# Seven products for eight in four of the eleven pairs of the last matrix product

## The chip, the cores and the metric

The kernel runs on one core of a Trainium2 chip. The metric is the device time of one execution in microseconds (us). TensorE (PE) multiplies; VectorE (DVE), ScalarE (ACT) and GpSimd (POOL) work on elements; SyncE (SP) issues most transfers.

## The reference

A trunk of two layers on 256 tokens of 1024 features, in float32. Each layer is half a SwiGLU step, a mixer, and another half step; at the end stands an RMS norm:

```python
def swiglu(h, w_gate, w_up, w_down):
    return (jax.nn.silu(h @ w_gate) * (h @ w_up)) @ w_down
...
    for layer in range(DEPTH):
        h = h + FFN_RESIDUAL_WEIGHT * swiglu(rmsnorm(h, ffn1_norm[layer]), ...)
        hn = rmsnorm(h, mix_norm[layer])
        ...
        h = h + FFN_RESIDUAL_WEIGHT * swiglu(rmsnorm(h, ffn2_norm[layer]), ...)
        ...
    return rmsnorm(h, final_norm)
```

The hidden width of SwiGLU is 2816 = 22 blocks of 128. The change concerns the last `swiglu` of layer 1 and its product with `w_down`, which is (256 x 2816) times (2816 x 1024).

## The kernel before, in words

**Numbers in two parts.** TensorE takes operands in a shorter format (`F32R`). So each operand is split: ScalarE copies it to a high part (`wh`, or half 0 of an `act` tile), VectorE subtracts that from the original for the low part (`wl`, half 1). A product is then three matmuls, high by high, high by low and low by high (`product`), or, for gate, up and the earlier down products, a wide matmul of 512 columns and a narrow one of 256 (`products_t`).

**Stages.** The stages follow each other: SwiGLU, mixer A, SwiGLU, SwiGLU, mixer B, SwiGLU, norm. Within the last SwiGLU (names `f21`), `ffn_blocks` goes over the 22 hidden blocks, two at a time. For each two it loads 1 MB of gate and 1 MB of up weights (`unit`: one transfer into a `raw` tile, then two high and two low tiles of 128 x 1024), and for each block it runs gate and up products and then closes the block before: join the two halves of the accumulator (ScalarE copy and VectorE add, `joined`), scale by the norm's row (VectorE for gate, GpSimd for up, L355), silu (ScalarE), multiply (L356), split into an `act` tile (`parts_of`). A list `beside` can hold calls that are put ahead of a double block.

**The last product.** `down_last` has the activations as the stationary operand and the weights as the moving one, so its result stands with tokens on the partitions. Two halves of 128 tokens (`t`) by two halves of 512 features (`c`) give four accumulators. It goes over 11 pairs of hidden blocks: one transfer of two rows of blocks (2 x 128 x 1024), split as above, then for each of two blocks k, each t and each c one product: eight products, 24 matmuls of 512 columns for a pair. The last two pairs (four blocks) are held back, so that the accumulators end one after the other: for each (t, c) the four blocks' products, then half of the result is added to the residual stream `h` (L432) and its squares and scaled outputs are begun (`finish_part`). The last accumulator is cut into two of 256 columns, the second of them called `end`.

**The residual stream** is kept with features on the partitions (`hT`). Ahead of `down_last` it is turned: 16 transposes of 128 x 128 on TensorE (L694) through three PSUM tiles (`trt`), and four ScalarE copies into `h[t][c]` (L695).

**What sets the order.** Each engine runs its own instructions in the order in which they are issued; a scheduler places them when the program is built, so this order is not quite that of the source. Buffers are pools: four `raw` tiles, eight tiles each of `wh` and `wl` (128 x 1024), 22 tiles "a" (`act` among them), five accumulators (`acc`) and three PSUM tiles (`trt`). A transfer waits until its `raw` tile has been split; a split waits until TensorE has read the part tile whose place it takes.

Of the kernel before, what the change touches and what calls it, by code (L numbers as in the profile page):

```python
# [25 lines left out]
NG = H // HG  # L26
ROT = 16
HALF = ROT // 2
LEAD = 4
EPS = 1e-6  # L30
SCALE = DH ** -0.5
# [31 lines left out]
def trunk(ctx: ExitStack, tc: tile.TileContext, a: dict, out: bass.AP):  # L63
# [13 lines left out]
    def atile(shape, dt=F32, name="a"):  # L77
        return ap_.tile(shape, dt, tag="a", name=name)

    def acc(name):  # L80
        return accp.tile([P, 512], F32, tag="acc", name=name)

    def flat(ap):
        return ap.rearrange("p c n -> p (c n)")

    def parts_of(hi, lo, src, scale=1.0, later=None):

        def rest():
            if isinstance(scale, float):
                nc.vector.tensor_sub(lo, src, hi.bitcast(F32))  # L90
# [9 lines left out]
    def trt(name):  # L100
        return trp.tile([P, 512], F32, tag="tr", name=name)
# [40 lines left out]
    def unit(name, k, n, srcs):  # L142

        raw = rawp.tile([P, k, n], F32, tag="raw", name=f"raw_{name}")
        for dst, src in srcs:
            nc.sync.dma_start(raw if dst is None else raw[:, :, dst], src)
        return pieces_of(name, raw, k, n)
# [28 lines left out]
    def rows(w, k0, k, c0, n):  # L176
        return w[k0 * P:(k0 + k) * P, c0:c0 + n].rearrange("(k p) n -> p k n", p=P)

    def product(accs, xh, xl, ws, first, last):

        for ac, (wh, wl) in zip(accs, ws):
            nc.tensor.matmul(ac, xh, wh, start=first, stop=False)  # L182
        for ac, (wh, wl) in zip(accs, ws):
            nc.tensor.matmul(ac, xh, wl, start=False, stop=False)  # L184
        for ac, (wh, wl) in zip(accs, ws):
            nc.tensor.matmul(ac, xl, wh, start=False, stop=last)  # L186
# [94 lines left out]
    class Pieces:  # L281
# [55 lines left out]
        nc.vector.tensor_add(s, ac[:, :S], s)  # L337
        return s

    def ffn_blocks(name, wg, wu, norm, first=None, beside=()):  # L340

        blocks = []

        def both(f, pair):
            acs = [acc(f"{name}_{n}{f}") for n in "gu"]
            cols = slice(f % 2 * P, (f % 2 + 1) * P)
            products_t(acs, [[(wh[:, cols], wl[:, cols]) for wh, wl in w] for w in pair], norm.x, True, True)
            return acs

        def close(f, gate, up):  # L350
            g = joined(gate, f"{name}_g{f}")
            nc.vector.tensor_mul(g, g, norm.row)  # L352
            nc.scalar.activation(g, g, AF.Silu)  # L353
            u = joined(up, f"{name}_u{f}")
            nc.gpsimd.tensor_tensor(u, u, norm.row, op=ALU.mult)  # L355
# [49 lines left out]
        down_t(name, wd, blocks, after)  # L405


    def down_last(name, w, nk, blocks, h, weight, part, after, tail=4):


        accs = [[acc(f"dn_{name}_{t}_{c}") for c in range(2)] for t in range(NT)]
        held = []

        def cut(ws, cols):
            return tuple(w[:, cols] for w in ws)

        halves = [slice(c * 512, (c + 1) * 512) for c in range(2)]
        for u in range(nk // 2):
            for i, ws in enumerate(unit(f"{name}_{u}", 2, D, [(None, rows(w, 2 * u, 2, 0, D))])):
                k = 2 * u + i  # L420
                if k < nk - tail:
                    for t in range(NT):
                        product(accs[t], *blocks[t][k], [cut(ws, half) for half in halves], k == 0, False)
                else:
                    held.append((k, ws))
        for t in range(NT):
            for c, half in enumerate(halves):
                n = 512 if (t, c) != (1, 1) else S
                for k, ws in held:
                    product([accs[t][c][:, :n]], *blocks[t][k], [cut(ws, slice(half.start, half.start + n))], False,  # L430
                            k == nk - 1)
                nc.vector.scalar_tensor_tensor(h[t][c], accs[t][c], weight, h[t][c], op0=ALU.mult, op1=ALU.add)  # L432
                part(t, slice(half.start, half.start + n))
            if t:
                end = acc(f"dn_{name}_end")[:, :S]
                for k, ws in held:
                    product([end], *blocks[t][k], [cut(ws, slice(D - S, D))], k == nk - tail, k == nk - 1)
                hc = h[1][1][:, S:]
                nc.vector.scalar_tensor_tensor(hc, end, weight, hc, op0=ALU.mult, op1=ALU.add)
                part(t, slice(D - S, D), True)  # L440
            after(t)

    def out_t(name, pieces, base, blocks, norm, tail=3):
# [224 lines left out]
    def ending(at):  # L668
# [18 lines left out]
    blocks = ffn_blocks("f21", a["ffn2_w_gate"][1], a["ffn2_w_up"][1], n6)  # L687

    h = [[xp.tile([P, 512], F32, tag=f"kx{2 * t + c}", name=f"h_{t}_{c}") for c in range(2)] for t in range(NT)]
    for t in range(NT):  # L690
        for c in range(2):
            tr = trt(f"h_{t}_{c}")
            for k in range(4):
                nc.tensor.transpose(tr[:, k * P:(k + 1) * P], hT[:, 4 * c + k, t * P:(t + 1) * P], ident)  # L694
            nc.scalar.activation(h[t][c], tr, AF.Copy)  # L695

    parts = [[], []]
    outs = [[None, None] for t in range(NT)]
# [26 lines left out]
    def finish(t):  # L725
# [8 lines left out]
    down_last("f21_d", a["ffn2_w_down"][1], KF,  # L734
              [[tuple(x[:, i, t * P:(t + 1) * P] for i in range(2)) for x in blocks] for t in range(NT)],
              h, 0.5, finish_part, finish)


_INS = ["ffn1_w_gate", "ffn1_w_up", "ffn1_w_down", "ffn2_w_gate", "ffn2_w_up", "ffn2_w_down",
# [23 lines left out]
```

## Time and profile before

| | |
|---|---|
| time, median of 3 runs | 990.88 us (990.67 to 990.91) |
| the profiled execution's own time | 990.92 us |
| its span, first to last instruction | 989.1 us |
| mean granted TensorE clock | 1.000 |
| 11 loads of the last product | 1024 KB each, 4.9 us from issue to landing (median) |
| HBM traffic | 177 GB/s over the span |

The lines of the profile are read so: a line number, an engine, an operation, the tile written and the tiles read with their numbers left out (so `f21_d` is shown as `f_d`), and the shape as partitions x elements. In a group, what follows the bar is the busy time, the mean length of one in ns, and the engine's idle time just before with what ended it. In a timeline the first column is the start and the second the length in us. Matmuls are pipelined: the length of one is longer than the distance to the next.

### The profile page before, as it was taken

To read this page: it belongs to the slowest core of one execution; us is meant where nothing else is said; L and a number is where in the kernel's file an instruction comes from. 1 tells how busy PE (TensorE), PEld (TensorE's weight loads), DVE (VectorE), ACT (ScalarE), POOL (GpSimd) and SP (SyncE) were. 2 spreads that over 40 slices of the span, in tenths; PEclk is the share of its full clock that TensorE was granted. 3 is DMA by queue.
4 is the path that set the end of the run, shared out by engine and by line. 5 is a ranking of instruction groups with operands and counts; after the bars stand their busy time and mean duration, and the time that the engine had idled before them with its cause. 6 is when DMAs were issued, how large, how long until landed. Compare 5 with 4: busy or idle time off the path is not lost.

```text
span 989.1 us, 15227 instructions
## 1 busy us (share of the span) xinstructions
PE 976.2 (99%) x5652; PEld 849.5 (86%) x5652; DVE 729.4 (74%) x1291; ACT 586.1 (59%) x1073; POOL 170.1 (17%) x194
## 2 busy tenths in 40 slices
PE   8999999999999999999999999999999999999997
PEld 5888888888889888888888888888888998888886
DVE  6987866677887788776678877656678878888642
ACT  7656654467776665655456566545577756665531
POOL 3211111122302211110112111101143022111000
PEclk9999999999999999999999999999999999999999
DMA  9776565655433566565655665665534345655611
GB/s 303 246 256 204 169 210 185 213 171 171 128 117 125 171 187 206 178 200 181 212 171 172 198 191 185 202 202 190 194 128 128 120 141 173 207 174 201 202 62 43
DMA packets 152395, 176.03 MB, mean 178 GB/s; under 512 B 3584, under 2 KB 140288, under 8 KB 152320
## 3 DMA queue, kind: packets, MB, share of 16 engines
q1 hardware_dynamic: 151600, 174.24, 55.1%
q8 instruction: 44, 0.72, 0.3%
q10 hardware_dynamic: 720, 0.82, 0.2%
q14 instruction: 31, 0.25, 0.1%
HBM read 173.99 MB, written 1.05 MB: 177 GB/s over the span
## 4 chain that ended last, share of the span: by engine, by line
PE 68%; DVE 2%; ACT 2%; issue 1%; POOL 0%; POOLq 0%; ACTq 0%; DVEq 0%
PE f_g L193 12%; PE f_u L193 12%; PE dn_f L193 8%; PE f_u L196 6%; PE f_g L196 6%; PE dn_f L196 4%; PE dn_f_d L186 2%; PE dn_f_d L182 2%; PE dn_f_d L184 2%; PE q_b L182 1%; PE kv_b L182 1%; PE q_b L186 1%; PE kv_b L186 1%; PE kv_b L184 1%; PE q_b L184 1%
## 5 line engine op out<-in xcount | busy, mean ns | idle before, releaser
L193 PE MATMUL f_g<-x_n,wh_f_g 128*128 128x512 f32 x688 | 180.1, 394 | 0.0
L193 PE MATMUL f_u<-x_n,wh_f_u 128*128 128x512 f32 x688 | 177.3, 390 | 0.0
L193 PEld LDWEIGHTS f_u<-x_n,wh_f_u 128*128 128x128 f32 x688 | 129.1, 188 | 27.3
L193 PEld LDWEIGHTS f_g<-x_n,wh_f_g 128*128 128x128 f32 x688 | 124.1, 189 | 22.7
L355 POOL TENSOR_TENSOR j_f_u<-j_f_u,r_n 128x256 f32<-128x256 f32 x88 | 77.6, 884 | 377.9 <-DVE j_f_u L337 355.5
L193 PE MATMUL dn_f<-act_f,wh_f 128*128 128x512 f32 x528 | 126.5, 391 | 0.0
L157 DVE TENSOR_TENSOR wl_f_u<-raw_f_u,wh_f_u 128x1024 fp32r<-128x1024 f32 x86 | 119.6, 1393 | 1.5 <-ACT wh_f_u L156 1.4
L157 DVE TENSOR_TENSOR wl_f_g<-raw_f_g,wh_f_g 128x1024 fp32r<-128x1024 f32 x86 | 103.6, 1235 | 15.1 <-PE f_g L196 10.7
L193 PEld LDWEIGHTS dn_f<-act_f,wh_f 128*128 128x128 f32 x528 | 96.8, 188 | 18.6
L157 DVE TENSOR_TENSOR wl_f<-raw_f,wh_f 128x1024 fp32r<-128x1024 f32 x72 | 81.8, 1153 | 35.6 <-ACT wh_f L156 26.7
L196 PE MATMUL f_u<-x_n,wl_f_u 128*128 128x256 f32 x688 | 103.3, 283 | 0.0
L196 PE MATMUL f_g<-x_n,wl_f_g 128*128 128x256 f32 x688 | 102.9, 282 | 0.0
L196 PEld LDWEIGHTS f_g<-x_n,wl_f_g 128*128 128x128 f32 x688 | 96.5, 190 | 6.3
L156 ACT ACTIVATE wh_f<-raw_f 128x1024 fp32r<-128x1024 f32 x72 | 67.3, 979 | 49.4 <-PE dn_f L193 27.1
L156 ACT ACTIVATE wh_f_g<-raw_f_g 128x1024 fp32r<-128x1024 f32 x86 | 89.4, 1049 | 11.2 <-issue 6.0
L156 ACT ACTIVATE wh_f_u<-raw_f_u 128x1024 fp32r<-128x1024 f32 x86 | 86.6, 1047 | 15.2 <-PE f_g L193 10.9
L196 PEld LDWEIGHTS f_u<-x_n,wl_f_u 128*128 128x128 f32 x688 | 91.6, 192 | 0.0
L230 POOL TENSOR_TENSOR ss_n<-ss_n,sq_n 128x256 f32<-128x256 f32 x42 | 41.9, 999 | 244.2 <-ACT sq_n L229 243.3
L94 ACT ACTIVATE act_f<-j_f_g 128x256 fp32r<-128x256 f32 x88 | 36.5, 417 | 72.1 <-DVE j_f_g L356 71.8
L353 ACT ACTIVATE j_f_g<-j_f_g 128x256 f32<-128x256 f32 x88 | 36.8, 418 | 67.1 <-DVE j_f_g L352 66.6
L196 PEld LDWEIGHTS dn_f<-act_f,wl_f 128*128 128x128 f32 x528 | 68.1, 191 | 2.8
L196 PE MATMUL dn_f<-act_f,wl_f 128*128 128x256 f32 x528 | 69.0, 283 | 0.0
(220 smaller groups left out, 1702.3 us busy)
## 6 DMA issues: line engine op xcount, KB each, us to landing
raw_f_g<-in_ffn_w_gate_dram SPq DMA_DIRECT2D x43, 1024.0 KB, 5.4
raw_f_u<-in_ffn_w_up_dram SPq DMA_DIRECT2D x43, 1024.0 KB, 5.3
raw_f<-in_ffn_w_down_dram SPq DMA_DIRECT2D x24, 1024.0 KB, 5.1
raw_f_d<-in_ffn_w_down_dram SPq DMA_DIRECT2D x11, 1024.0 KB, 4.9
raw_f<-in_ffn_w_down_dram SPq DMA_DIRECT2D x12, 768.0 KB, 4.5
raw_qka<-in_a_w_qkv_dram SPq DMA_DIRECT2D x16, 512.0 KB, 4.3
raw_va<-in_a_w_qkv_dram SPq DMA_DIRECT2D x4, 1024.0 KB, 5.1
raw_ao<-in_a_w_o_dram SPq DMA_DIRECT2D x4, 1024.0 KB, 4.9
```

Source lines behind the costliest of these rows:

```text
L94: nc.scalar.activation(hi, src, AF.Copy, scale=scale)
L156: nc.scalar.activation(wh, r, AF.Copy)
L157: nc.vector.tensor_sub(wl, r, wh.bitcast(F32))
L182: nc.tensor.matmul(ac, xh, wh, start=first, stop=False)
L184: nc.tensor.matmul(ac, xh, wl, start=False, stop=False)
L186: nc.tensor.matmul(ac, xl, wh, start=False, stop=last)
L193: nc.tensor.matmul(ac, wh, flat(x), start=first and i == 0, stop=False)
L196: nc.tensor.matmul(ac[:, :S], wl, x[:, 0, :], start=False, stop=last and i == len(ws) - 1)
L230: nc.gpsimd.tensor_tensor(self.ss, self.ss, sq, op=ALU.add)
L353: nc.scalar.activation(g, g, AF.Silu)
L355: nc.gpsimd.tensor_tensor(u, u, norm.row, op=ALU.mult)
```

## The change

Four of the eleven pairs (2, 4, 6 and 7, `FAST`) are computed by seven products of quarters instead of eight. The left factor of a pair is the 2 x 2 of its two hidden blocks and two halves of tokens; the right factor is the 2 x 2 of two hidden blocks and two halves of features. Four sums of activations (`quarter_sums`: two 128 x 256 operations in one, two of 128 x 128, all on VectorE, then a split of 128 x 512) are made in the gate/up stage, one double block after their activations. Four sums of weights are made when the pair is loaded: two on VectorE in one operation of 1024 columns (`ac`), two on GpSimd of 512 columns (`b`, and `d` from it), into tiles of their own (`ac` in a tile that mixer B's keys had, `b` and `d` in tiles that the gate/up stage's inputs `x` had). The pair then needs four tiles of high and low parts instead of two (`a` to `d`; `b` with one quarter only). Three of the seven products go straight into the accumulators 11, 12 and 21; the others into m1, m5, m6 and m7, which are kept over the four pairs and combined once, behind the last of them, by `collect` (one ScalarE, six VectorE and two GpSimd operations on 128 x 512), into `h`. That makes eight PSUM tiles: five `acc` and three `trt`.

For that reason, and since `trt` is then taken, the turning of `h` is moved: each of its four groups of four transposes is put ahead of one double block of gate/up (f = 4, 6, 8 and 10), through `beside`.

The order within a plain pair is one product after another, where before the two halves of features went through the three parts side by side. Pair i + 1 is loaded and split ahead of the products of pair i in the source.

```diff
+FAST = (2, 4, 6, 7)
...
+    def quarter_sums(x, hi, lo, name):
+        q = atile([P, 4, P], name=f"q_{name}")
+        x = x.rearrange("p a (t n) -> p (a t) n", n=P)
+        nc.vector.tensor_sub(q[:, :2], x[:, 0::3], x[:, 1:2].to_broadcast([P, 2, P]))
+        nc.vector.tensor_add(q[:, 2], q[:, 1], x[:, 0])
+        nc.vector.tensor_sub(q[:, 3], x[:, 2], q[:, 2])
+        rest = []
+        parts_of(hi, lo, flat(q), later=rest.append)
+        return rest
...
-            nc.vector.tensor_mul(g, g, u)
+            nc.vector.tensor_mul(prod, g, u)
             x = atile([P, 2, S], F32R, name=f"act_{name}_{f}")
-            parts_of(x[:, 0], x[:, 1], g)
+            parts_of(x[:, 0], x[:, 1], prod)
+            while rest:
+                rest.pop(0)()
+            if prod is not g and f % 2:
+                rest.extend(quarter_sums(pairs.pop(pair), *sums[pair], f"{name}_{f}"))
...
+        def load(i):
+            raw = rawp.tile([P, 4, 512], F32, tag="raw", name=f"raw_{name}_{i}")
+            nc.sync.dma_start(raw.rearrange("p (k c) n -> p k (c n)", k=2), rows(w, 2 * i, 2, 0, D))
+            if i not in sums:
+                return split(f"{i}a", raw[:, :2]) + split(f"{i}b", raw[:, 2:])
+            n = 2 * (sorted(sums).index(i) % 4)
+            ac = ap_.tile([P, 2, 512], F32, tag="qkl", name=f"sum_{name}_{i}ac", bufs=2)
+            b, d = [xp.tile([P, 1, 512], F32, tag=f"x{n + j}", name=f"sum_{name}_{i}{'bd'[j]}") for j in range(2)]
+            nc.vector.tensor_add(ac, raw[:, 0::3], raw[:, 1:2].to_broadcast([P, 2, 512]))
+            nc.gpsimd.tensor_tensor(b[:, 0], ac[:, 0], raw[:, 3], op=ALU.add)
+            nc.gpsimd.tensor_tensor(d[:, 0], b[:, 0], raw[:, 2], op=ALU.add)
+            b11, b21 = split(f"{i}a", raw[:, 0::2])
+            b22, = split(f"{i}b", raw[:, 3:])
+            ta, tc = split(f"{i}c", ac)
+            tb, td = split(f"{i}d", b, d)
+            return b11, b21, b22, ta, tc, tb, td
+
+        def fast(i, ws):
+            ...
+            for n, ac, left, right in (("1", m1, x[0][0], b11), ("11", c11, x[0][1], b21), ("12", c12, l3, b22),
+                                       ("5", m5, l5, ta), ("7", m7, l7, tc), ("6", m6, l6, tb),
+                                       ("21", c21, x[1][1], td)):
+                add(n, ac, left, right, last and len(n) == 1)
+
+        def collect():
+            a, b, c, d = [atile([P, 512], name=f"co_{name}_{n}") for n in "abcd"]
+            nc.scalar.activation(a, m1, AF.Copy, scale=weight)
+            nc.vector.scalar_tensor_tensor(b, m6, weight, a, op0=ALU.mult, op1=ALU.subtract)
+            nc.gpsimd.tensor_tensor(h[0][0], h[0][0], a, op=ALU.add)
+            nc.vector.scalar_tensor_tensor(c, m7, weight, b, op0=ALU.mult, op1=ALU.subtract)
+            nc.vector.scalar_tensor_tensor(b, m5, -weight, b, op0=ALU.mult, op1=ALU.add)
+            nc.gpsimd.tensor_tensor(h[0][1], h[0][1], b, op=ALU.add)
+            nc.vector.scalar_tensor_tensor(d, m5, -weight, c, op0=ALU.mult, op1=ALU.subtract)
+            nc.vector.tensor_add(h[1][0], h[1][0], c)
+            nc.vector.tensor_add(h[1][1], h[1][1], d)
+
+        ahead, held = [load(0)], []
+        for i in range(pairs):
+            if i + 1 < pairs:
+                ahead.append(load(i + 1))
+            ws = ahead.pop(0)
+            if i in sums:
+                fast(i, ws)
+                if i == max(sums):
+                    collect()
+            elif i < pairs - tail:
+                for k in range(2):
+                    for t in range(NT):
+                        for c in range(2):
+                            add(*quarters[t][c], blocks[t][2 * i + k], ws[2 * k + c])
+            else:
+                held += [(2 * i + k, ws[2 * k:2 * k + 2]) for k in range(2)]
...
+    turns = [lambda t=t, c=c: turn_h(t, c) for t in range(NT) for c in range(2)]
+    blocks = ffn_blocks("f21", a["ffn2_w_gate"][1], a["ffn2_w_up"][1], n6, beside=[lambda: None] + turns, sums=sums)
```

In the order of the program as built, these things stand by engine around the last product: on GpSimd, the sums b of pair 2, b of pair 4, d of pair 2 and d of pair 4 come ahead of the last gate/up multiplication (L355 of the kernel before); on VectorE, the sum `ac` of pair 2 comes ahead of the splits of pair 0, the last gate/up product ahead of the low parts of pair 2's b and d, and `collect`'s operations behind the splits of pair 10.

More of the change, by code (lines that the diff above doesn't have):

```diff
@@ L338, in joined, with ffn_blocks @@
         return s
-    def ffn_blocks(name, wg, wu, norm, first=None, beside=()):
-        blocks = []
+    def quarter_sums(x, hi, lo, name):
[7 more added lines that the diff above has]
+        return rest
+    def ffn_blocks(name, wg, wu, norm, first=None, beside=(), sums=None):
+        blocks, pairs, rest = [], {}, []
         def both(f, pair):
@@ L355, in close @@
             nc.gpsimd.tensor_tensor(u, u, norm.row, op=ALU.mult)
-            nc.vector.tensor_mul(g, g, u)
-            x = atile([P, 2, S], F32R, name=f"act_{name}_{f}")
-            parts_of(x[:, 0], x[:, 1], g)
+            pair = f // 2
+            if sums is not None and pair in sums:
+                if f % 2 == 0:
+                    pairs[pair] = atile([P, 2, S], name=f"act2_{name}_{f}")
+                prod = pairs[pair][:, f % 2]
+            else:
+                prod = g
+            nc.vector.tensor_mul(prod, g, u)
+            x = atile([P, 2, S], F32R, name=f"act_{name}_{f}")
+            parts_of(x[:, 0], x[:, 1], prod)
[3 more added lines that the diff above has]
+                rest.extend(quarter_sums(pairs.pop(pair), *sums[pair], f"{name}_{f}"))
             blocks.append(x)
@@ L405, in ffn, with down_last, add, split @@
         down_t(name, wd, blocks, after)
[L408 to L421, printed above, removed]
-                    for t in range(NT):
-                        product(accs[t], *blocks[t][k], [cut(ws, half) for half in halves], k == 0, False)
-                else:
-                    held.append((k, ws))
+    def down_last(name, w, blocks, sums, h, weight, part, after, tail=2):
+        c11, c12, c21, m1, m5 = [acc(f"dn_{name}_{n}") for n in ("11", "12", "21", "m1", "m5")]
+        c22, m6, m7 = [trt(f"dn_{name}_{n}") for n in ("22", "m6", "m7")]
+        begun = set()
+        def add(n, ac, x, ws, last=False):
+            product([ac], *x, [ws], n not in begun, last)
+            begun.add(n)
+        def split(n, *srcs):
+            k = sum(src.shape[1] for src in srcs)
+            wh, wl = [wp.tile([P, k, 512], F32R, tag=tag, name=f"{tag}_{name}_{n}") for tag in ("wh", "wl")]
+            at = 0
+            for src in srcs:
+                part = slice(at, at + src.shape[1])
+                nc.scalar.activation(wh[:, part], src, AF.Copy)
+                nc.vector.tensor_sub(wl[:, part], src, wh[:, part].bitcast(F32))
+                at = part.stop
+            return [(wh[:, i, :], wl[:, i, :]) for i in range(k)]
+        def load(i):
[15 more added lines that the diff above has]
+        def fast(i, ws):
+            b11, b21, b22, ta, tc, tb, td = ws
+            l7, l5, l6, l3 = [tuple(v[:, j * P:(j + 1) * P] for v in sums[i]) for j in range(4)]
+            x = [[blocks[t][2 * i + k] for k in range(2)] for t in range(NT)]
+            last = i == max(sums)
+            for n, ac, left, right in (("1", m1, x[0][0], b11), ("11", c11, x[0][1], b21), ("12", c12, l3, b22),
[13 more added lines that the diff above has]
+            nc.vector.tensor_add(h[1][1], h[1][1], d)
+        quarters = [[("11", c11), ("12", c12)], [("21", c21), ("22", c22)]]
+        pairs = KF // 2
+        ahead, held = [load(0)], []
[9 more added lines that the diff above has]
+                for k in range(2):
+                    for t in range(NT):
+                        for c in range(2):
+                            add(*quarters[t][c], blocks[t][2 * i + k], ws[2 * k + c])
+            else:
+                held += [(2 * i + k, ws[2 * k:2 * k + 2]) for k in range(2)]
+        end = acc(f"dn_{name}_end")[:, :S]
@@ L426, in down_last @@
         for t in range(NT):
-            for c, half in enumerate(halves):
-                n = 512 if (t, c) != (1, 1) else S
+            for c in range(2):
+                n, ac = quarters[t][c]
+                cut = 512 if (t, c) != (1, 1) else S
                 for k, ws in held:
[L430 to L433, printed above, removed]
+                    add(n, ac[:, :cut], blocks[t][k], tuple(v[:, :cut] for v in ws[c]), k == KF - 1)
+                nc.vector.scalar_tensor_tensor(h[t][c], ac, weight, h[t][c], op0=ALU.mult, op1=ALU.add)
+                part(t, slice(c * 512, c * 512 + cut))
@@ L434, in down_last @@
             if t:
-                end = acc(f"dn_{name}_end")[:, :S]
                 for k, ws in held:
-                    product([end], *blocks[t][k], [cut(ws, slice(D - S, D))], k == nk - tail, k == nk - 1)
+                    add("end", end, blocks[t][k], tuple(v[:, S:] for v in ws[1]), k == KF - 1)
                 hc = h[1][1][:, S:]
                 nc.vector.scalar_tensor_tensor(hc, end, weight, hc, op0=ALU.mult, op1=ALU.add)
-                part(t, slice(D - S, D), True)
+                part(t, slice(512 + S, 1024), True)
@@ L686, in trunk, with turn_h @@
           a["b_w_o"][0], masks[:, 1, :], n6)
-    blocks = ffn_blocks("f21", a["ffn2_w_gate"][1], a["ffn2_w_up"][1], n6)
-    h = [[xp.tile([P, 512], F32, tag=f"kx{2 * t + c}", name=f"h_{t}_{c}") for c in range(2)] for t in range(NT)]
[L690 to L695, printed above, removed]
+    sums = {}
+    for n, i in enumerate(FAST):
+        if n < 2:
+            sums[i] = tuple(xp.tile([P, 512], F32R, tag=f"kx{4 + 2 * n + j}", name=f"left_{i}_{j}") for j in range(2))
+        else:
+            parts = ap_.tile([P, 2, 512], F32R, tag="qkh", name=f"left_{i}", bufs=2)
+            sums[i] = (parts[:, 0], parts[:, 1])
+    h = [[xp.tile([P, 512], F32, tag=f"kx{2 * t + c}", name=f"h_{t}_{c}") for c in range(2)] for t in range(NT)]
+    def turn_h(t, c):
+        tr = trt(f"h_{t}_{c}")
+        for k in range(4):
+            nc.tensor.transpose(tr[:, k * P:(k + 1) * P], hT[:, 4 * c + k, t * P:(t + 1) * P], ident)
+        nc.scalar.activation(h[t][c], tr, AF.Copy)
+    turns = [lambda t=t, c=c: turn_h(t, c) for t in range(NT) for c in range(2)]
+    blocks = ffn_blocks("f21", a["ffn2_w_gate"][1], a["ffn2_w_up"][1], n6, beside=[lambda: None] + turns, sums=sums)
     parts = [[], []]
@@ L732, in finish @@
             (nc.scalar, nc.sync)[c].dma_start(out[0, t * P:(t + 1) * P, c * 512:(c + 1) * 512], outs[t][c])
-    down_last("f21_d", a["ffn2_w_down"][1], KF,
+    down_last("f21_d", a["ffn2_w_down"][1],
               [[tuple(x[:, i, t * P:(t + 1) * P] for i in range(2)) for x in blocks] for t in range(NT)],
-              h, 0.5, finish_part, finish)
+              sums, h, 0.5, finish_part, finish)
 _INS = ["ffn1_w_gate", "ffn1_w_up", "ffn1_w_down", "ffn2_w_gate", "ffn2_w_up", "ffn2_w_down",
```

## The prediction

> **What bounds the kernel now.** I read the page's first, second and fourth parts, then the windows of the last two stages, then TensorE's timeline from gate/up into the last product.
>
> ```profile
> span 989.1 us, 15227 instructions
> ...
> PE 976.2 (99%) x5652; PEld 849.5 (86%) x5652; DVE 729.4 (74%) x1291; ACT 586.1 (59%) x1073; POOL 170.1 (17%) x194
> ...
> PEclk9999999999999999999999999999999999999999
> ...
> PE 68%; DVE 2%; ACT 2%; issue 1%; POOL 0%; POOLq 0%; ACTq 0%; DVEq 0%
> ```
>
> TensorE is busy 99% of the span at full granted clock, and the chain that ended last is TensorE's almost everywhere. A busy PE need not be fed at its peak, so I look at how closely its matmuls start. Two windows, the columns being PE, PEld, DVE, ACT and POOL busy time:
>
> ```profile
> 865.50:909.95 44.45, 44.45 (x258) 39.28 (x256) 35.07 (x57) 27.28 (x49) 6.10 (x8) 1.00 0.58 190
> ...
> 922.81:971.88 49.07, 49.07 (x219) 40.62 (x218) 21.03 (x20) 16.57 (x19) 0.79 (x1) 1.00 0.32 108
> ```
>
> The first is the last gate/up stage, with VectorE busy 35.07 of 44.45 us; the second is the last product, with VectorE only 21.03 of 49.07. The timeline (start, length):
>
> ```profile
> 920.12 1.12 PE L196 MATMUL f_u<-x_n,wl_f_u 128*128 128x256 f32 x8
> 921.09 1.96 PE L694 MATMUL h<-ident,hT 128*128 128x128 f32 x16
> 922.81 0.71 PE L182 MATMUL dn_f_d<-wh_f_d,act_f 128*128 128x512 f32 x2
> 923.36 0.62 PE L184 MATMUL dn_f_d<-wl_f_d,act_f 128*128 128x512 f32 x2
> ...
> 971.88 0.39 PE L182 MATMUL dn_f_d<-wh_f_d,act_f 128*128 128x512 f32 x1
> ...
> 980.04 0.28 PE L182 MATMUL dn_f_d<-wh_f_d,act_f 128*128 128x256 f32 x1
> ...
> 982.80 0.28 PE L186 MATMUL dn_f_d_end<-wh_f_d,act_f 128*128 128x256 f32 x1
> ```
>
> Between 971.88 and 980.04 stand the 36 wide matmuls of three held quarters (four blocks of k, three matmuls each): 8.16/36 = 0.2267 us apiece, with no gap. From 922.81 to 971.88 there are 216 matmuls: 0.2272 us apiece, so the whole stage starts matmuls at that rate. Only fewer matmuls, or a wait put between them, can move the end.
>
> **The removed products.** A plain pair is eight products of three matmuls, 24 x 0.2267 = 5.44 us; a pair by seven products is 21 x 0.2267 = 4.76. Four such pairs save 12 matmuls: the changed program's order has 252 where this one has 264 in the last product. **Term: -2.72 us.** Stationary blocks change with every matmul in both, and the rate of the held part is already that of one product after another, so I take no change in rate.
>
> **The turns.** The 16 transposes are not removed; they move in four groups of four between gate/up matmuls. In the old place the low gate/up products end at 920.12 + 8 x 0.12 = 921.08, the transposes hold TensorE until 922.81, and the first two wide matmuls take 0.55 instead of 0.45: 1.83 us. For a group of four among wide matmuls the trace has this, in mixer B:
>
> ```profile
> 703.64 0.39 PE L186 MATMUL kv_b<-wh_kvb,x_kx 128*128 128x512 f32 x1
> 703.88 0.60 PE L601 MATMUL qt_b<-ident,rt_b 128*128 128x128 f32 x4
> 704.23 0.48 PE L182 MATMUL kv_b<-wh_kvb,x_kx 128*128 128x512 f32 x1
> 704.54 0.40 PE L184 MATMUL kv_b<-wl_kvb,x_kx 128*128 128x512 f32 x1
> ```
>
> From 703.64 to 704.54 is 0.90 us, of which two matmuls are 0.45: 0.45 us for a group, 1.79 for four. **Term: -0.04, taken as 0**; bounds -0.4 (only the 0.35 from 703.88 to 704.23 counts) and +0.4 (the slow first matmul twice). The four copies to h (L695 below, 0.61 each) go into ScalarE's gate/up time, where it is busy 27.28 of 44.45.
>
> **What VectorE, ScalarE and GpSimd get instead.**
>
> ```profile
> L157 DVE TENSOR_TENSOR wl_f_d<-raw_f_d,wh_f_d 128x1024 fp32r<-128x1024 f32 x22 | 27.8, 1272 | 21.5 <-ACT wh_f_d L156 19.7 <-PE f_g L196 1.8
> ...
> L156 ACT ACTIVATE wh_f_d<-raw_f_d 128x1024 fp32r<-128x1024 f32 x22 | 22.8, 1055 | 21.7 <-PE dn_f_d L186 21.7
> ...
> L432 DVE SCALAR_TENSOR_TENSOR h<-dn_f_d,h 128x512 f32<-128x512 f32 x4 | 2.7, 686 | 12.6 <-PE dn_f_d L186 12.6
> ...
> L695 ACT ACTIVATE h<-h 128x512 f32<-128x512 f32 x4 | 2.1, 607 | 0.0
> ```
>
> ```profile
> 33.32 0.41 DVE L90 TENSOR_TENSOR act_f<-j_f_g,act_f 128x256 fp32r<-128x256 f32 x1
> 33.66 1.21 DVE L157 TENSOR_TENSOR wl_f_u<-raw_f_u,wh_f_u 128x1024 fp32r<-128x1024 f32 x1
> ...
> 133.31 0.68 DVE L157 TENSOR_TENSOR wl_f<-raw_f,wh_f 128x512 fp32r<-128x512 f32 x1
> ...
> 897.58 2.36 DVE L157 TENSOR_TENSOR wl_f_g<-raw_f_g,wh_f_g 128x1024 fp32r<-128x1024 f32 x2 [0.91 <-PE f_g L196]
> ...
> 911.99 1.76 DVE L157 TENSOR_TENSOR wl_f_d<-raw_f_d,wh_f_d 128x1024 fp32r<-128x1024 f32 x1
> ```
>
> ```profile
> 33.55 1.93 POOL L355 TENSOR_TENSOR j_f_u<-j_f_u,r_n 128x256 f32<-128x256 f32 x1 [3.57 <-DVE j_f_u L337]
> ...
> 911.88 0.79 POOL L355 TENSOR_TENSOR j_f_u<-j_f_u,r_n 128x256 f32<-128x256 f32 x1 [5.45 <-DVE j_f_u L337]
> 916.83 0.74 POOL L355 TENSOR_TENSOR j_f_u<-j_f_u,r_n 128x256 f32<-128x256 f32 x1 [4.16 <-DVE j_f_u L337]
> ```
>
> In the last product VectorE keeps its 22 low parts of 1024 and gets 12 more of 512 (0.68), four sums of 1024 (1.21) and six steps of collect (0.69): 8.2 + 4.8 + 4.1 = 17 us, on a stage where it has 28 us free of 49. ScalarE gets 12 x 0.61 = 7 us, with 32 free. GpSimd gets ten sums of 512 columns, a size that no row of its adds has: twice the quiet 256 row is 1.48 us, twice the worst 3.86; I take 1.48, the nearest quiet one.
>
> Totals don't decide; due times do. With the turns moved, TensorE enters the last product at about 922.9 as before and reaches pair 2 at 933.75, pair 3 at 938.5, 4 at 943.95, 5 at 948.7, 6 at 954.15, 7 at 958.9, 8 at 963.7, the held four at 969.1.
>
> *Pair 2.* Its sums b and d go into tiles that the gate/up inputs x occupy until the last low products, 920.12 + 1.79 + 0.28 = 922.2. On GpSimd four sums (b of 2, b of 4, d of 2, d of 4) stand ahead of the last up block's multiplication, and on VectorE the product with it stands ahead of the low parts of b and d. Walk: 922.2 + 4 x 1.48 + 0.79 + 0.42 + 2 x 0.68 = 930.7. TensorE uses them from the sixth product, 933.75 + 5 x 0.68 = 937.15: 6.4 us early. So this added wait is hidden.
>
> *Pairs 6 and 7* stand side by side. There are eight tiles of high and of low parts and such a pair fills four; taken in turn, 7's last (b, d) needs the tile that pair 5's second half leaves at 954.15. With 2 x 0.61 on ScalarE and 0.68 on VectorE behind it that is 956.1, used at 958.9 + 3.4 = 962.3: 6 us early.
>
> *Collect* stands behind the last splits on VectorE (about 963.5) and takes 4.1 us: 967.6, before the first closing step at 969.1 + 2.72 = 971.8. Nothing else is queued behind it.
>
> *Gate/up.* Each of four double steps gets 0.42 + 2 x at most 0.42 + 0.68 = 1.9 us of VectorE, on 8.8 of 11.1 busy: just inside, and the weights that VectorE splits at 897.58 are first used in their low part one block (8 x 2 x (0.2267 + 0.12) = 5.55) and one row of low products (0.96) before 920.12, at 913.6, so a slip of some microseconds is covered. The sum for pair 2 stands on VectorE ahead of the split of pair 0 and waits for pair 2's load. That load:
>
> ```profile
> 888.83 53.38 SPq L146 DMA_DIRECT2D raw_f_d<-in_ffn_w_down_dram  x11
> ```
>
> ```profile
> raw_f_d<-in_ffn_w_down_dram SPq DMA_DIRECT2D x11, 1024.0 KB, 4.9
> ```
>
> It can be issued once the last gate block is split (897.58 + 2.36, 1.8 later now), so it lands near 907, and pair 0's split, which comes one double step (11.1) after 897.58 at 908.7, has until 922.9. SyncE's issues keep their order.
>
> **Sum.** The profiled run took 990.92 for a span of 989.1 (1.82 around it) and lies 0.04 above the median. Span 989.1 - 2.72 - 0.04 = 986.3, plus 1.82: **988.2 us**. The tail behind the last matmul, 982.80 to the end, is untouched.
>
> **Rivals.**
>
> *No gain: GpSimd's sums hold VectorE up.* For it: at 911.99 a 1.21 low part took 1.76 while GpSimd's 0.79 ran. The Trainium skill, page "SBUF — State Buffer", section "SBUF: two separate sides", says that GpSimd and a VectorE operation with two SBUF inputs share one port pair as an exclusive lock, so that one fully blocks the other. The trace agrees at 33.55: GpSimd's 0.74 became 1.93, ending 0.6 after VectorE's two operations. With full exclusion, VectorE's work from 922 until the last low part (18 x 1.23 + 12 x 0.68 + 2 x 1.21 + six closing steps of 0.42 = 35.2) and GpSimd's nine operations (8 x 1.48 + 0.79 = 12.6) come to 47.8 us, and the last low part is due at 969.1 + 3 x 0.68 = 971.1, 49 after: each microsecond that VectorE waits for a tile then shows once 1.3 us are used up. With 2 to 3 such microseconds the loss is 1 to 2: **989.2 to 990.2**. Against: in the waits GpSimd runs, so they count once. Chance 0.13.
>
> *Slower: the four sums ahead of VectorE's product.* Every 0.1 us more for one of them makes pair 2's b, d parts 0.4 later; from 1.48 + 6.4/4 = 3.1 us for a sum TensorE waits. At twice the worst row, 3.86, it waits 3.1 (990.92 - 2.76 + 3.1 = 991.3); where VectorE's operations overtake each sum three times (1.48 + 3 x 1.21 = 5.1) it waits 4 x 2.0 = 8: **996.2**. For: at 33.55 two VectorE operations went first. Against: VectorE itself stops for GpSimd at that product, and only 3.5 us of its operations (two low parts of 1024, one of 512, one 0.42) stand before it, so all four sums together lose that much, and 6.4 are there. Chance 0.10.
>
> *The edit doesn't bite*: excluded as to counts (252 matmuls), so 0.01, inside the first rival.
>
> **How the numbers follow.** Forecast 0.76, with its own range 987.7 to 988.9 (turns -0.4 to +0.4, some tenths of waits). A measurement of this kernel tells 0.2%, 1.98 us, from no change: 988.90 and 992.86. Faster 0.76 is the forecast; same 0.14 the first rival and the milder half of the stall; slower 0.10 the second. The range that holds 8 in 10 is 987.6 to 990.4: the forecast and most of the first rival.
>
> **Right or wrong by the next profile.** Right: twelve fewer matmuls from the same start near 922.8, last matmul near 980.1, pairs by seven products 4.76 us long, no start of TensorE later than 0.3 us after the one before; GpSimd sums of 512 below 3.1 us. Wrong: a hole in TensorE at pair 2's sixth product (first place to look), at pair 6 or 7, or gate/up stretched beyond the 1.8 us of the turns.

## The result, and the profile after

The changed kernel takes 988.31 us (median; 987.41 to 989.41) against 990.88 for the kernel before on the same chip: ratio 0.997, 95% interval 0.9962 to 0.9979. The forecast was 988.2; that the median lies 0.1 from it is closer than an interval of some 0.8 us either way can vouch for. The profiled execution took 988.49 us for a span of 986.7, so what lies around the span is 1.8 us as before.

First the page after: span, busy time by engine, and the share of the chain that ended last.

```profile
span 986.7 us, 15270 instructions
...
PE 974.5 (99%) x5640; PEld 847.9 (86%) x5640; DVE 755.7 (77%) x1329; ACT 594.3 (60%) x1090; POOL 200.5 (20%) x204
...
PE 68%; DVE 2%; ACT 2%; issue 1%; POOL 0%; POOLq 0%; ACTq 0%; DVEq 0%
```

There are 12 matmuls fewer (5640 for 5652), and the chain is still TensorE's: VectorE gained 26 us and GpSimd 30, and neither share of the chain moved. The timeline gives the ends of the last product (start, length, engine):

```profile
923.21 0.40 PE L183 MATMUL dn_f_d<-wh_f_d_0a,act_f 128*128 128x512 f32 x1
...
980.39 0.28 PE L187 MATMUL dn_f_d_end<-wh_f_d_10b,act_f 128*128 128x256 f32 x1
```

From first matmul to last it is 980.39 - 923.21 = 57.18 us, with no matmul later than its turn. Before it was 982.80 - 922.81 = 59.99. The last stage's length fell by 2.81, while its end moved by 2.41, since the stage starts 0.40 later. Where two profiles are compared, lengths say more than ends: their earlier, unchanged stages differ by some tenths too. From the last matmul to the end it is 6.31 us (before 6.30).

What the other engines do meanwhile, in windows (columns PE, PEld, DVE, ACT and POOL busy, granted clock, DMA share, GB/s): the last gate/up stage, and the last product up to the first held quarter.

```profile
865.50:909.95 44.45, 44.45 (x258) 39.27 (x257) 37.41 (x65) 27.09 (x51) 7.59 (x9) 1.00 0.58 183
923.21:969.35 46.14, 46.14 (x206) 38.20 (x205) 44.27 (x44) 25.19 (x33) 27.72 (x11) 1.00 0.33 115
```

VectorE is now busy 44.27 of 46.14 us there, where before it was 21.03 of 49.07. The forecast had given it 17 more, about 38; the rest is in operations that became longer. GpSimd's timeline shows why:

```profile
922.62 1.30 POOL L467 TENSOR_TENSOR sum_f_d_2b<-sum_f_d_2ac,raw_f_d 128x512 f32<-128x512 f32 x1 [0.49 <-PE f_u L197]
923.87 1.48 POOL L467 TENSOR_TENSOR sum_f_d_4b<-sum_f_d_4ac,raw_f_d 128x512 f32<-128x512 f32 x1
925.32 2.26 POOL L468 TENSOR_TENSOR sum_f_d_2d<-sum_f_d_2b,raw_f_d 128x512 f32<-128x512 f32 x1
927.54 1.74 POOL L468 TENSOR_TENSOR sum_f_d_4d<-sum_f_d_4b,raw_f_d 128x512 f32<-128x512 f32 x1
...
936.03 11.37 POOL L467 TENSOR_TENSOR sum_f_d_6b<-sum_f_d_6ac,raw_f_d 128x512 f32<-128x512 f32 x1 [4.41 <-DVE sum_f_d_6ac L466]
947.48 2.15 POOL L468 TENSOR_TENSOR sum_f_d_6d<-sum_f_d_6b,raw_f_d 128x512 f32<-128x512 f32 x1
```

A sum of 512 columns takes 1.30 us undisturbed and 1.48 to 2.26 beside VectorE. Pair 6's sum b took 11.37. VectorE's timeline over that time:

```profile
935.81 1.22 DVE L454 TENSOR_TENSOR wl_f_d_3b<-raw_f_d,wh_f_d_3b 128x1024 fp32r<-128x1024 f32 x1
...
945.57 0.68 DVE L454 TENSOR_TENSOR wl_f_d_6b<-raw_f_d,wh_f_d_6b 128x512 fp32r<-128x512 f32 x1
946.97 1.51 DVE L454 TENSOR_TENSOR wl_f_d_6c<-sum_f_d_6ac,wh_f_d_6c 128x1024 fp32r<-128x1024 f32 x1 [0.72 <-ACT wh_f_d_6c L453]
948.41 1.77 DVE L454 TENSOR_TENSOR wl_f_d_6d<-sum_f_d_6b,wh_f_d_6d 128x512 fp32r<-128x512 f32 x1
950.33 1.56 DVE L454 TENSOR_TENSOR wl_f_d_6d<-sum_f_d_6d,wh_f_d_6d 128x512 fp32r<-128x512 f32 x1
```

Eleven operations ran back to back from 935.81 to about 946.25; the sum had started 0.22 us into the first. There VectorE stood idle for 0.72 us, waiting for ScalarE, and 1.15 us after 946.25 the sum was done. In the other direction the low parts of pair 6 took 1.77 and 1.56 instead of 0.68. None of it reached TensorE: pair 6's second low part is done at 951.89, and the first product that uses these parts starts at 957.92, 6.0 us later.

### The profile page after: what moved, and what is told of

Same layout as the page of the kernel before. It is cut to its first block, busy times and chain, and to the rows that moved or that the text cites. A ratio compares the mean times of both kernels' runs of the same rounds, so it can differ in the third digit from the quotient of the medians.

```text
span 986.7 us, 15270 instructions
## 1 busy us (share of the span) xinstructions
PE 974.5 (99%) x5640; PEld 847.9 (86%) x5640; DVE 755.7 (77%) x1329; ACT 594.3 (60%) x1090; POOL 200.5 (20%) x204
## 4 chain that ended last, share of the span: by engine, by line
PE 68%; DVE 2%; ACT 2%; issue 1%; POOL 0%; POOLq 0%; ACTq 0%; DVEq 0%
PE f_g L194 12%; PE f_u L194 12%; PE dn_f L194 8%; PE f_u L197 6%; PE f_g L197 6%; PE dn_f L197 4%; PE dn_f_d L187 1%; PE dn_f_d L185 1%; PE dn_f_d L183 1%; PE q_b L183 1%; PE kv_b L183 1%; PE q_b L187 1%; PE q_b L185 1%; PE kv_b L187 1%; PE kv_b L185 1%
## 5 line engine op out<-in xcount | busy, mean ns | idle before, releaser
L370 POOL TENSOR_TENSOR j_f_u<-j_f_u,r_n 128x256 f32<-128x256 f32 x88 | 81.9, 933 | 373.9 <-DVE j_f_u L338 351.5
L95 ACT ACTIVATE act_f<-j_f_g 128x256 fp32r<-128x256 f32 x80 | 33.2, 417 | 66.2 <-DVE j_f_g L378 65.9
```

## The experiments

Every kernel is compared with the kernel before on its own chip, whose medians were 991.03 us for the first four, 991.06 for the next four and 991.88 for the last. So ratios, not microseconds, compare kernels of different groups. "Last product" is the time from its first matmul to its last. "b and d of pair 2" are its two sums of weights on GpSimd.

**Only the moved turns.**

```diff
-FAST = (2, 4, 6, 7)
+FAST = ()
```

> No pair is made by seven products; the turning of h is still moved into gate/up, and the last product still goes one product after another. Theory A (only the count of matmuls matters): 264 matmuls in the last product, so the time of the kernel before to 0.1 us (turns -0.04), within 0.3 us with noise. Theory B (the new place of the turns or the new order of products gives part of the 2.6 us): 0.5 us or more faster than before.

Measured 991.14 us, ratio 1.0002 (0.9993 to 1.001); the last product's ends in its timeline:

```profile
923.14 0.40 PE L183 MATMUL dn_f_d<-wh_f_d_0a,act_f 128*128 128x512 f32 x1
...
983.04 0.28 PE L187 MATMUL dn_f_d_end<-wh_f_d_10b,act_f 128*128 128x256 f32 x1
```

That is 59.90 us, as before to 0.09. The turns and the new order within a plain pair neither gain nor lose what can be measured (the interval is some 0.9 us either way). The gain belongs to the pairs.

**Two pairs instead of four.**

```diff
-FAST = (2, 4, 6, 7)
+FAST = (2, 6)
```

> Pairs 2 and 6 by seven products instead of four pairs. Theory A: 6 matmuls fewer, 6 x 0.2267 = 1.36 us faster than before. Theory C (GpSimd's and VectorE's added work takes something back from each such pair, which the four-pair kernel hides in its noise): the gain is not in proportion, more than 1.6 or less than 1.1 us.

Measured 989.74 us, ratio 0.9986 (0.9977 to 0.9995), 1.29 less than before; the last product took 58.54 us = 59.90 - 1.36. Each pair is worth three matmuls, 0.68 us, and nothing is held back.

**The sums b and d on VectorE.**

```diff
-            nc.gpsimd.tensor_tensor(b[:, 0], ac[:, 0], raw[:, 3], op=ALU.add)
-            nc.gpsimd.tensor_tensor(d[:, 0], b[:, 0], raw[:, 2], op=ALU.add)
+            nc.vector.tensor_add(b[:, 0], ac[:, 0], raw[:, 3])
+            nc.vector.tensor_add(d[:, 0], b[:, 0], raw[:, 2])
```

> Four pairs as in the changed kernel, but the eight sums b and d on VectorE instead of GpSimd. Theory A: VectorE has 5 to 6 us in hand at every part; it gets 8 x 0.68 = 5.4 us more and loses the waits that GpSimd's sums cause, so TensorE sees no wait and the time is that of the changed kernel, 2.7 us faster than before. Theory C (the shared port costs time on the path): 0.5 us or more faster than the changed kernel. Theory D (VectorE is already at its limit): slower than the changed kernel by 0.5 us or more, with a hole in TensorE at pair 6 or 7.

Measured 988.18 us, ratio 0.9971 (0.9959 to 0.9982), and the last product 57.18 us, as in the changed kernel. The window of the same length as above:

```profile
923.49:969.63 46.14, 46.14 (x206) 38.20 (x205) 42.13 (x52) 25.16 (x33) 4.25 (x3) 1.00 0.34 115
```

VectorE takes over eight sums and is yet 2.1 us less busy (42.13 for 44.27), because nothing stretches its other operations. So GpSimd's sums cost VectorE more than they take from it. TensorE's time does not show it either way: the mutual waits cost nothing on the path in this kernel.

**A fifth pair.**

```diff
-FAST = (2, 4, 6, 7)
+FAST = (2, 4, 6, 7, 8)
...
+            else:
+                sums[i] = tuple(pp.tile([P, 512], F32R, tag="pT", name=f"left_{i}_{j}") for j in range(2))
```

> Pairs 2, 4, 6, 7 and 8 by seven products. Theory A: 15 matmuls fewer, 3.40 us faster than before, since VectorE has done pair 7 about 6 us ahead and gets 3.2 us more for pair 8; collect then ends behind the first held quarter's products, which delays only its closing steps. Theory D (VectorE at its limit): a hole in TensorE at pair 8 or at the held blocks, gain below 2.7 us.

Measured 988.24 us, ratio 0.997 (0.9959 to 0.998), no more gain than with four pairs. The last product did fall by 0.68, to 56.50, without a hole; but the tail behind the last matmul grew from 6.31 to 6.82 us. The chain that ended last, in order of time (start, length, what):

```profile
936.36 11.37 POOL sum_f_d_6b L467
947.81 2.15 POOL sum_f_d_6d L468
949.99 0.64 ACT wh_f_d_6d L453
950.65 1.50 DVE wl_f_d_6d L454
952.16 2.30 DVE wl_f_d_7a L454
...
967.07 1.14 DVE wl_f_d_10a L454
...
969.26 0.69 DVE co_f_d_b L489
...
973.24 0.68 DVE h L496
973.92 0.61 DVE h L523
```

The starved sum of pair 6 now stands on the path. Through VectorE's queue of splits it moves `collect` back, and `collect` ends at 973.92, though the first held quarter's last matmul starts at 971.26 and TensorE waits for nothing. In the changed kernel VectorE had stood idle 2.7 us ahead of that first closing step.

**Five pairs, with the sums b and d on VectorE:** the edits of the last two together.

> Pairs 2, 4, 6, 7 and 8 by seven products, and all sums b and d on VectorE. The kernel with five pairs and GpSimd's sums was 0.68 us shorter on TensorE than with four, but its tail was 0.5 us longer, and its chain began at GpSimd's sum b of pair 6, which took 11.4 us. Theory C2 (that sum's wait for VectorE's port is what the tail pays): without GpSimd's sums VectorE is through collect early enough, the tail is 6.3 us again, and the time is 3.4 us below before. Theory D (VectorE has simply too much work): the tail stays 0.5 us or more too long, 2.9 us below before or less.

Measured 987.97 us, ratio 0.9966 (0.9953 to 0.9978): the lowest ratio of all. The last product took 56.50 us and the tail 6.32 again. So the tail's half microsecond came from GpSimd's sums. The intervals of this version and of the changed kernel overlap; that it is the faster of the two rests on the two traces (0.68 us shorter from first matmul to last with the same tail), not on the times. Against the kernel before it is faster beyond its interval.

**Pair 2's sum b made four times.**

```diff
-            nc.gpsimd.tensor_tensor(b[:, 0], ac[:, 0], raw[:, 3], op=ALU.add)
+            for _ in range(4 if i == 2 else 1):
+                nc.gpsimd.tensor_tensor(b[:, 0], ac[:, 0], raw[:, 3], op=ALU.add)
```

> The changed kernel with GpSimd's sum b of pair 2 made four times instead of once (the same values each time). In the order as built, two of the three added operations stand ahead of the last gate/up multiplication, and sum d behind it. The prediction's second rival: TensorE waits only once pair 2's parts are late by more than the time in hand, which the profile of the changed kernel gives as 5.1 us (first part of d ready 932.7, used 937.7). Two to three operations of 1.3 to 1.7 us and sum d behind the multiplication add 4 to 6: a hole of 0 to 1 us at pair 2's sixth or seventh product, the time 0 to 1 us above the changed kernel. If GpSimd's work had no way to TensorE at all, no hole and no change; if there were no time in hand, a hole of 4 us or more.

Measured 988.6 us, ratio 0.9973 (0.9961 to 0.9984), last product 57.18 without a hole. Sum d of pair 2 ended at 935.02 where it had ended at 927.58: 7.4 us later. But VectorE's low parts, which had waited for GpSimd's last gate/up multiplication in any case, came only about 3.2 later (the first starts at 935.2 for 932.00), inside the 5.1 us that were in hand. Behind TensorE it did show: the tail grew from 6.31 to 6.78 us (span 987.3, last matmul at 980.52). Pair 7's sum b took 7.97 us in this run, and `collect` kept VectorE until 974.69, about 2 us after the first held quarter's products were there.

**Seven times** (the same edit with 7 for 4).

> The same with six added operations; three of them stand between the last gate/up multiplication and sum d. Second rival: sum d ends near 940, its low part is there near 941.2, used at 938.4 without a wait: a hole of 2 to 4 us at pair 2's seventh product and nowhere else, so the time is about that of the kernel before (gain 0 +- 1 us). If the other pairs have no time in hand for a VectorE that runs 8 us later, further holes and a time 2 us or more above before.

Measured 994.17 us, ratio 1.0029 (1.0019 to 1.0038): slower than before by 3.1 us. A hole at pair 2 alone was expected to bring no change, give or take 1 us, and only further holes 2 us or more above before. TensorE's timeline at pair 2's sixth and seventh products, and behind it:

```profile
937.20 0.39 PE L187 MATMUL dn_f_d_m<-wh_f_d_2c,left 128*128 128x512 f32 x1
938.38 0.50 PE L183 MATMUL dn_f_d_m<-wh_f_d_2d,left 128*128 128x512 f32 x1 [0.79 <-ACT wh_f_d_2d L453]
939.62 0.50 PE L185 MATMUL dn_f_d_m<-wl_f_d_2d,left 128*128 128x512 f32 x1 [0.74 <-DVE wl_f_d_2d L454]
...
941.36 0.80 PE L185 MATMUL dn_f_d<-wl_f_d_2d,act_f 128*128 128x512 f32 x1 [0.55 <-DVE wl_f_d_2d L454]
...
942.38 0.63 PE L183 MATMUL dn_f_d<-wh_f_d_3a,act_f 128*128 128x512 f32 x1
942.80 0.63 PE L185 MATMUL dn_f_d<-wl_f_d_3a,act_f 128*128 128x512 f32 x1
```

The holes are at pair 2 alone, and of the size worked out: starts later than a matmul's 0.2267 by 0.95, 1.01 and 0.94 us, 2.9 together. But the last product is 63.02 us, 5.84 longer than 57.18. The other half comes behind the holes, where matmuls that wait for nothing start 0.43 apart. Windows of the same run (the last but two numbers of a line is the granted clock):

```profile
937.00:941.30 4.30, 2.28 (x7) 0.84 (x5) 2.94 (x4) 3.60 (x5) 1.94 (x2) 0.87 0.24 39
941.30:947.00 5.70, 5.64 (x13) 4.51 (x14) 3.65 (x5) 4.79 (x7) 1.15 (x1) 0.50 0.93 341
947.00:955.00 8.00, 8.00 (x36) 6.56 (x35) 8.00 (x7) 4.80 (x6) 2.63 (x2) 1.00 0.40 131
```

In the middle window the clock granted was 0.50 of full: 13 matmuls where the changed kernel has 27 in the same window. In windows of 1 us the lower clock reaches from about 940.2 to 947.0, 6.8 us. All nine executions of this kernel took 993.29 us or more, about 2 us above what the holes alone make (991.06 - 2.72 + 2.90 = 991.2), so there the lower clock cost something each time.

**The four pairs side by side.**

```diff
-FAST = (2, 4, 6, 7)
+FAST = (2, 3, 4, 5)
```

> Four pairs by seven products side by side: 2, 3, 4 and 5 instead of 2, 4, 6 and 7. Theory A alone (the count of matmuls): 2.72 us below before, as with the changed kernel. Theory A with due times: VectorE's 5.7 us and more for such a pair stand against TensorE's 4.76 three times in a row, and GpSimd's sums for pairs 4 and 5 find no gap; a walk by the lengths of the changed kernel's rows has the last parts of pairs 4 and 5 ready within 1 us of their use, so holes of 0 to 1.5 us at pair 5, and 1 to 2.7 us below before.

Measured 990.77 us, ratio 0.9998 (0.9989 to 1.0007): between 1.1 us below and 0.7 above the kernel before, so most or all of the gain is gone; 1 to 2.7 below was expected. In the profiled execution the last product took 61.08 us. TensorE's timeline, and the windows:

```profile
943.51 0.50 PE L185 MATMUL dn_f_d<-wl_f_d_3d,act_f 128*128 128x512 f32 x1 [0.46 <-DVE wl_f_d_3d L454]
...
945.74 0.50 PE L185 MATMUL dn_f_d_m<-wl_f_d_4a,act_f 128*128 128x512 f32 x1 [1.26 <-DVE wl_f_d_4a L454]
```

```profile
942.00:946.40 4.40, 2.68 (x11) 1.61 (x10) 4.40 (x4) 3.43 (x5) 2.52 (x2) 1.00 0.00 0
946.40:950.00 3.60, 3.60 (x11) 2.79 (x10) 3.60 (x5) 2.11 (x2) 0.00 (x0) 0.53 0.71 208
```

VectorE is late with the low parts of pairs 3 and 4, not of pair 5 as expected: starts slip by 0.62 and 1.43 us, 2.05 together. In those splits it works beside GpSimd's sums:

```profile
939.97 1.77 DVE L454 TENSOR_TENSOR wl_f_d_3d<-sum_f_d_3b,wh_f_d_3d 128x512 fp32r<-128x512 f32 x1
941.67 1.78 DVE L454 TENSOR_TENSOR wl_f_d_3d<-sum_f_d_3d,wh_f_d_3d 128x512 fp32r<-128x512 f32 x1
943.38 2.30 DVE L454 TENSOR_TENSOR wl_f_d_4a<-raw_f_d,wh_f_d_4a 128x1024 fp32r<-128x1024 f32 x1
```

They take 1.77, 1.78 and 2.30 instead of 0.68, 0.68 and 1.21. That is 3.3 us lost in three operations just ahead of the late parts, more than the 2.05 that TensorE waited. So by these rows the mechanism of the first rival decides in this order, and the places of the pairs, 2, 4, 6 and 7, keep it off the path. It is argued, not shown: no run has this order with the sums on VectorE, and VectorE's mere amount of work remains a rival.

Again a stretch at half the clock follows, 3.4 us long (946.6 to 950.0). But the times say that it doesn't follow in each execution. Six of the ten took 990.36 to 990.86 us, about what the holes alone make (991.06 - 2.72 + 2.05 = 990.4); four took 992.12 to 993.03, the profiled one (992.12) among them.

**Seven times, with the idle time filled.** Is the lower clock a consequence of the holes, or of something else in that stretch?

```diff
+                for _ in range(14 if i == 2 and n == "6" else 0):
+                    nc.tensor.matmul(c11, fill[:, :P], fill, start=False, stop=False)
```

(`fill` is all zero by then, so these matmuls add nothing.)

> The changed kernel with pair 2's sum b made seven times, as in the run that came to 994.17 us, and fourteen matmuls with an all-zero tile (128x512, adding nothing to the sum) put ahead of pair 2's sixth product, where TensorE stood idle in that run. There it had three holes of 0.95, 1.01 and 0.94 us, together 2.9, and the last product took 63.02 us from first matmul to last, 5.84 more than the changed kernel's 57.18; from 941.3 to 947.0 the granted clock was 0.50. Theory H (the holes brought the lower clock down): the fourteen fillers take 14 x 0.2267 = 3.17 us, TensorE has no hole and the granted clock stays at 1.00, the last product takes 57.18 + 3.17 = 60.35 us, and the time is 988.31 + 3.2 = 991.5 (990.7 to 992.5). Rival I (the slow matmuls come from something else in that stretch, such as the seven sums, the splits behind them or the transfers at 0.93 of the DMA engines' time): the stretch at 0.50 stays, the last product takes about 63 us or more, and the time is 993.5 to 994.8.

Measured 992.41 us, ratio 1.0009 (1.0 to 1.0019); by ratio 2.0 us less than without the filling, though TensorE has 14 matmuls more to do.

```profile
937.00:941.30 4.30, 4.23 (x20) 2.35 (x20) 2.51 (x3) 3.18 (x5) 2.37 (x2) 1.00 0.16 22
941.30:947.00 5.70, 5.70 (x26) 4.51 (x26) 3.78 (x4) 5.70 (x8) 0.85 (x1) 1.00 0.95 338
```

The clock stays at 1.00 over the same sums, the same splits behind them and transfers as dense (0.95 for 0.93). So the sums, the splits and the transfers do not bring it down by themselves, and the rival falls: the holes did. The times agree: without the filling all nine executions took 993.29 us or more, with it all but one of the ten 993.18 or less. The last product took 61.53 us and not 60.35, because in this run one more hole of 1.04 us came at pair 4, where VectorE, behind in its work, was late with a low part that took 2.31 beside GpSimd. After that single hole the clock stayed at full.

## Why the prediction was right, point by point

- **Twelve matmuls, -2.72 us.** Right. The last product is 2.81 shorter than before and 2.72 shorter than with the turns alone (59.90 to 57.18). Two pairs gave 1.36 and five 3.40 in the last product, so the term is counted in matmuls, as the forecast did.
- **The turns, taken as 0.** Right within what can be measured: 1.0002 (0.9993 to 1.001) with them alone. The second of the four groups, in the timeline:

```profile
832.81 0.60 PE L789 MATMUL h<-ident,hT 128*128 128x128 f32 x4
833.16 2.09 PE L194 MATMUL f_g<-x_n,wh_f_g 128*128 128x512 f32 x8
```

  The transposes hold TensorE for 0.35 us, and the matmul behind adds about a tenth, as in the mixer's rows that served as the price.
- **GpSimd's sums, 1.48 us each.** Undersized, without consequence. Undisturbed one takes 1.30, less than the forecast; beside VectorE the first four took 1.30, 1.48, 2.26 and 1.74, together 6.78 instead of 5.92; one took 11.37, outside the bounds of 1.48 to 3.86 and above the 3.1 that the forecast named as a sign of being right. The bound was taken from rows in which at most two of VectorE's operations went first; here eleven did. That it cost nothing was luck in the order: with a fifth pair a sum of the same 11.37 us stands in the chain whose tail is 0.5 longer.
- **Pair 2's b and d, 6.4 us in hand.** Right in kind; 5.1 were there (the first low part ends at 932.68 and is used at 937.74). TensorE did not see three more sums, and did see six.
- **Pairs 6 and 7, 6 us in hand.** Right for pair 7, for which it was worked out, in the way it was worked out: ScalarE's part for the last sums waits until 954.80 for the tile that pair 5 leaves, the last low part is done at 957.07 (956.1 in the walk) and used from 962.68, 5.6 later. Pair 6 had 6.0 us in hand, but there the starved sum came last, which the walk had not foreseen.

```profile
954.80 0.63 ACT L453 ACTIVATE wh_f_d_7d<-sum_f_d_7b 128x512 fp32r<-128x512 f32 x1 [1.69 <-PE dn_f_d L187]
...
956.39 0.68 DVE L454 TENSOR_TENSOR wl_f_d_7d<-sum_f_d_7d,wh_f_d_7d 128x512 fp32r<-128x512 f32 x1
```

- **`collect` 4.2 us ahead of its use.** 2.7 were left. VectorE came to it 1.6 us later than in the walk, and one of its steps took 1.40 beside GpSimd. This was the step closest to failing: it is what the fifth pair used up, and three more sums too. The forecast's own sums had it as the smallest of the three margins, but no rival was built on it. Its last step and the first closing step:

```profile
969.07 0.68 DVE L496 TENSOR_TENSOR h<-h,co_f_d_d 128x512 f32<-128x512 f32 x1
972.47 0.69 DVE L523 SCALAR_TENSOR_TENSOR h<-dn_f_d,h 128x512 f32<-128x512 f32 x1 [2.72 <-PE dn_f_d L187]
```

- **Gate/up fits.** Right: VectorE 37.41 of 44.45, and the last product starts 0.40 later, of which 0.34 stands already ahead of that stage.
- **The first rival** (GpSimd's sums hold VectorE up) has the mechanism right and the place of its decision wrong for this order. The Trainium skill, page "SBUF — State Buffer", section "SBUF: two separate sides", says that whichever starts first, GpSimd's instruction or VectorE's with two SBUF inputs, has the shared ports for its whole instruction, while the other blocks. The rows agree: the low part of 948.41 took 1.77 us for 0.68, ending 0.55 after the sum that ran since 947.48. That a sum waits for more than the one operation it met is what the 11.37 us add.
- **The second rival** (the sums ahead of VectorE's last gate/up product) was priced for holes alone. Seven sums of b gave holes of the size worked out, 2.9 us, and then cost as much again through the clock. Its 991.3 had no term for that.

## What to carry to other kernels

Where TensorE's starts stand one matmul apart, fewer matmuls are a gain that can be counted, as long as every operand's due time is walked through and not only the totals of each engine. Keep sums off GpSimd when VectorE has a long queue of operations with both inputs in SBUF: here they cost VectorE more than making them itself (busy 44.27 us against 42.13), and one can stand still until VectorE idles or takes an input from PSUM. And price a short wait of TensorE at up to twice its length: here holes of 2 to 3 us within 4.5 us cost about twice themselves in both profiled executions, though in one of the two kernels, by its times, not in most of the others.

## What the runs showed of the hardware that was not expected

**A GpSimd operation can lose again and again.** One sum of 1.30 us stood for 11.37 us behind eleven back-to-back operations of VectorE, and finished 1.15 us after VectorE first idled. With the fifth pair, GpSimd's add in `collect` likewise took 4.67 us, and with the pairs side by side 6.84, for 1.29 undisturbed. In these two VectorE did not idle: the add ended 1.2 us after VectorE began a step of `collect` that takes one of its inputs from PSUM (at 969.26 and 959.44). A full queue alone does not explain the loss. With three or six sums added, pair 6's sum b came 0.22 us into an operation of VectorE as here, the high parts for VectorE's next four operations were already made, and it took 2.15. What decides stays open.

**Short holes can halve the clock, and the same holes do not always.** In the last product three holes of about 1 us each within 4.4 us were followed by 6.8 us at 0.50; two of 0.62 and 1.43 within 3 us by 3.4 us; one of 1.04 by nothing. The kernels also have one hole of 1.5 us in common, in mixer A, far from the change. Here it is in the changed kernel, and with the sums b and d on VectorE, each with the window behind it:

```profile
284.48 0.36 PE L636 MATMUL po_a<-pT_a,vs_a 128*128 128x256 f32 x1 [1.50 <-DVE vs_a L93]
284.80:290.00 5.20, 5.05 (x42) 4.79 (x41) 4.83 (x9) 2.92 (x7) 0.00 (x0) 1.00 0.42 127
...
283.76 0.36 PE L636 MATMUL po_a<-pT_a,vs_a 128*128 128x256 f32 x1 [1.49 <-DVE vs_a L93]
284.80:290.00 5.20, 5.20 (x35) 5.20 (x33) 4.10 (x7) 2.18 (x6) 0.00 (x0) 0.67 0.57 179
```

A mean of 0.67 over 5.2 us is 3.4 us at 0.50. Of the eleven profiles, the kernel before included, three show this behind that hole (both kernels with all sums on VectorE, and the one with the idle time filled), and eight show 1.00 throughout. So the length of the holes alone does not decide. The Trainium skill, page "TensorE: Matmul & The Clock Gate", section "Why this matters for your kernels", asks for no idle gap over about 3 us between bursts of matmuls. The longest of these holes was about half of that, so the clock can fall after shorter waits than the rule names. What else decides, and where the threshold lies, these runs do not tell.
